# Causal attention products, a first phase without GpSimd and an early gate row in a hybrid decoder layer

## The chip, the cores and the metric

The kernel runs on one core of a Trainium2 chip. A core has five engines with a queue of instructions each: TensorE (PE, with PEld for its weight loads), VectorE (DVE), ScalarE (ACT), GpSimd (POOL) and SyncE (SP), which issues most transfers. Operands of the engines lie in SBUF; products are added up in PSUM. The metric is the device time of one execution in microseconds, the median of three runs; less is better.

## The reference

One decoder layer, 512 tokens by 1024 columns, float32:

```python
mod = silu(c) @ w_ada + b_ada
shift, scale, gate = split(mod, 3)
h = rmsnorm(x, g_pre) * (1 + scale) + shift
rq, rk, rv, rg, nq, nkv, ngl, ng = split(h @ w_in)
ret = groupnorm(retention(rotary(rq), rotary(rk), rv)) * silu(rg)     # 8 heads of 64
o_cmp = softmax(q @ kc.T, cmp_end <= tq) @ vc      # 31 compressed blocks
o_slc = softmax(q @ ks.T, tok <= tq) @ vs          # selected blocks
o_win = softmax(q @ kw.T, tq - 512 < kp <= tq) @ vw
att = (g0 * o_cmp + g1 * o_slc + g2 * o_win) * silu(ng)               # 8 heads of 64, 2 key groups
x + gate * rmsnorm(concat(ret, att) @ w_out, g_post)
```

With 512 tokens there are 8 blocks to select from and 16 may be taken, so the selected branch sees every key up to the query, as the window branch does.

## The kernel before

Every float32 operand of a large product is split into a high part `h` and a low remainder `l` that TensorE takes at full rate, and a product is three matrix multiplications: high by high, low by high, high by low. ScalarE makes the high part (a copy), VectorE or GpSimd the low one (a subtraction). So `wh_rg` and `wl_rg` are the halves of the weight `rg`, and `hh` and `hl` those of the transposed `h`.

The program is emitted by a list scheduler (`Plan`). The work stands in threads (`th_...`), each with a rank; of all that can go on, the one that can start first is emitted next. Ranks, prices and some choices of engine come from a table `T`. A step that names two engines goes to the one that the plan believes to be free sooner. Each engine then executes its own instructions in the order in which they were emitted and waits at semaphores where data or buffers are not ready. Every operation goes out through one helper, so nearly all rows name line 163 before the change and 174 after; the names of the tiles tell them apart.

The stages:

- First phase, to about 71 us. `th_ada(k)` sums column tile k of `w_ada` times silu(c) (`cs`) over eight row blocks (into `adac`, products on VectorE), transposes the sum on TensorE (`tp`), reduces it to two numbers a partition (`ab`, scale and shift); `th_prep(k)` transposes x and makes `hh` and `hl`; `th_nq_h` and `th_nq_l` multiply with the query weights (`nq`) and the weights of the compressed keys and values (`cc`). The low halves come from either GpSimd or VectorE, most from GpSimd, as do the last two steps of `ab`.
- Projections `rk`, `rv`, `rq` and `kv`, beside the two layers of compression (`w` tiles). Weights come in pieces of 256 KB through four raw buffers `wr`.
- Retention, beside the next projections.
- Attention. `th_unit(h, t)` takes query tile t of head h: scores `s` of both branches (keys `kT_h`, `kT_l`, queries `qs`; one more product with `idb` adds the causal mask `maskb`), the negated maximum `mx` on VectorE, the exponential `p` with its sum `den` on ScalarE, the division on GpSimd (`turn`), transposes on TensorE, and the split into the high and low tiles `pt..h`, `pt..l`. `th_pv(h)` multiplies these with the values `vst`, in halves of 256 queries, and with 32-row pieces of the compressed branch (`pcTh`, `pcTl`, made by `th_c`). The projections `rg` and `ng`, and later the output projection, fill TensorE between.
- The gate row. `th_gate` loads 16 pieces of `w_ada` (256 KB each) during attention into `misc`, multiplies and adds them into `gr` (GpSimd 13 times, VectorE otherwise); at the end one product with `ones` adds up the partitions.
- Output projection (`wo`, halves of `mr` for retention and `mn` for attention), root mean square, and the last additions, four query tiles one after the other.

Of the kernel before, what the change touches and what calls it, by code (L numbers as in the profile page):

```python
# [34 lines left out]
SEQ, D = 512, 1024  # L35
# [15 lines left out]
T = {'lat': 0.2, 'alt': 0.4, 'w': 1, 'post': 50, 'q': -1.8, 'var': 1.7, 'c': 1.6, 'cm': 2, 'pv': 4.5, 'gate': 300, 'kv0': 590.0, 'kv1': 105.89999999999999, 'rg': 108.5, 'ng': 601.4, 'stage': 3, 'cmp': 21, 'qs': 29.0, 'y': -0.8, 'n': -700, 'silu': 300, 'rows': 499, 'pm': 0.125, 'rgtag': 0, 'tags': 0, 'pact': 0.95, 'pv_': 1, 'pg': 1.0, 'trig': 15.0, 'ord': 0, 'att': 104.2, 'w1': 2, 'abe': 'g', 'wpre': 4, 'npj': (4, 0), 'x3': 0, 'sq3': 0, 'ada': ((0, 4, 5, 6, 7, 8), (0, 4, 6, 8), (0, 4, 8), (0, 4, 8)), 'sin': 40, 'al': 1.7, 'ld': 1, 'ad': -0.5, 'pr': 2.6, 'nh': 5.0, 'nl': 4, 'te': 'g', 'se': ('v', 'g'), 'a0': 2, 'raw': 0.12, 'half': 1, 'wg': 3}  # L51
# [6 lines left out]
class Plan:  # L58
    """A list scheduler for the order in which instructions are emitted.

    Work comes as threads: generators that yield what they need next. An engine's name (or several, to have the
    sooner one picked): the code up to the next yield emits for that engine. (get, resource, n): n free places.
    An event: that it has been set. Of all threads the one that can go on first does, the lower rank on a tie.
    """
# [3 lines left out]
    def __init__(self):  # L68
        self.cost, self.free, self.res, self.live, self.act_set = {}, {}, {}, [], None
        self.now, self.todo = 0.0, []  # L70

# [10 lines left out]
    def spawn(self, rank, gen):  # L82
        self.todo.append(("spawn", rank, gen))

# [64 lines left out]
class Engine:  # L149
    """An engine's instructions, with an estimate of what each costs for the plan."""  # L150
# [4 lines left out]
    def __getattr__(self, op):  # L155
        f = getattr(self.eng, op)

        def run(*a, **k):
            ins = [z.tensor.name for z in (*a[1:], *k.values()) if isinstance(z, bass.AP)]
            wait = T["raw"] if self.name != "pe" and self.out in ins else 0.0  # L160
            self.out = a[0].tensor.name
            self.plan.cost[self.name] = self.plan.cost.get(self.name, 0.0) + self.price(op, a, k) + wait
            return f(*a, **k)  # L163
# [6 lines left out]

def price_pe(op, a, k):
    if op == "transpose":
        return 128 * (2 if a[1].dtype == F32 else 1) / 2400
    n = size(a[2])
    if a[2].dtype == F32:
# [11 lines left out]
def price_v(op, a, k):  # L187
    n = size(a[1] if op == "tensor_reduce" else a[0])
    if op == "scalar_tensor_tensor":
        return 0.13 + n * 0.00104  # L190
    if op == "tensor_scalar" and a[1].tensor.name.split("_")[0] not in ("acc", "s", "tp", "pv"):
# [16 lines left out]
class Queue:  # L208
    """A DMA queue; plan.arrival is when the last transfer is done."""
# [13 lines left out]
def layer(ctx: ExitStack, tc: tile.TileContext, x, c, positions, w_ada, b_ada, g_pre, g_post,  # L223
# [51 lines left out]
    # ---------------------------------------------------------------- weights: float32 as hi + lo, in the order of use  # L275
# [28 lines left out]
    for k in range(KT):  # L304
        for nm, c0, n in (("nq", C_NQ, 512), ("cc", C_KV, 256)):
# [6 lines left out]
             (4, 6, 7, 8, 9, 10, 11, 12, 16, 17, 18, 19, 20, 21, 22, 23))[T["w1"]]  # L312
    for s_, (nm, u) in enumerate(MAIN):
# [13 lines left out]
    # ---------------------------------------------------------------- constants  # L327
# [5 lines left out]
    maskb, cmb, cm01 = ct("maskb", [128, 128], BF16), ct("cmb", [128, NT, 2, 32], BF16), ct("cm01", [128, 32])  # L333
# [5 lines left out]
    rs, rr = ct("rs", [128, NT, 8]), ct("rr", [40, SEQ], F32R)  # L339
    gr, sel = ct("gr", [128, D]), ct("sel", [128, 2])  # L340
# [7 lines left out]
    # =============================================================== adaLN, h, first projections  # L348
# [42 lines left out]
    for i in range(W_PRE):  # L391
# [22 lines left out]
    asel(cm01, [[-16, 32]], ALU.is_ge, 0.0, -31, 1)  # L414
    G.memset(sel, 1.0 / 64)
# [3 lines left out]
    # =============================================================== the work, as threads  # L419
    # The plan sets the order in which they are emitted.  # L420
# [9 lines left out]
    st = {}                                                    # tiles that threads share  # L430
# [1354 lines left out]
```

## Time and profile before

| | |
|---|---|
| runs, us | 394.85, 395.58, 395.92 (median 395.58) |
| span of the profiled execution, us | 392.6 |
| TensorE busy, us (share) | 369.7 (94%) |
| VectorE busy, us (share) | 290.4 (74%) |
| ScalarE busy, us (share) | 224.4 (57%) |
| GpSimd busy, us (share) | 198.8 (51%) |
| moved by DMA | 44.82 MB |

The profile shows one execution; its span, from the first to the last instruction, is 2.98 us less than the median of the runs, which holds what lies around it too. TensorE's records overlap, since its products are pipelined: how long a product occupies the engine is read from the start of one to the start of the next, not from the record's length. The chain of work that ended last is 77% TensorE.

### The profile page before, as it was taken

The numbers are of one execution on the slowest core, as the hardware profiler recorded it, in microseconds if no ns is written. First come the engines' busy times: TensorE is split into PE (matmuls) and PEld (weight loads), VectorE is DVE, ScalarE is ACT, GpSimd is POOL, SyncE is SP. The second block draws the span as 40 slices with busy tenths as digits, with TensorE's granted clock in tenths as the row PEclk, the third lists the DMA queues.
The fourth block names the chain that finished last, engine by engine and source line by source line (L and its number), as shares of the span: only waits on it lengthen the run. The fifth ranks groups of instructions, "written<-read, shape, count | busy, mean of one in ns | idle before, by whom it ended". The sixth has DMA issues, their size and how long they took to land.

```text
span 392.6 us, 7123 instructions
## 1 busy us (share of the span) xinstructions
PE 369.7 (94%) x2356; PEld 317.8 (81%) x2356; DVE 290.4 (74%) x643; ACT 224.4 (57%) x537; POOL 198.8 (51%) x332
## 2 busy tenths in 40 slices
PE   4879888999999999999999999999999999999993
PEld 1657666889999999999998888878888788777882
DVE  1598996799978756688978795488978876496532
ACT  5344545698555434367826583776786776583120
POOL 6565463214425317578735578888774443123200
PEclk9678998999999999999999999999999999999998
DMA  7999824433553454312112135423200000138341
GB/s 273 310 268 278 232 67 115 135 88 109 155 139 99 120 166 114 108 27 56 28 55 55 53 109 143 153 83 109 80 28 1 27 3 28 54 111 248 130 155 53
DMA packets 47084, 44.82 MB, mean 114 GB/s; under 512 B 5508, under 2 KB 39368, under 8 KB 47048
## 3 DMA queue, kind: packets, MB, share of 16 engines
q1 hardware_dynamic: 46984, 44.35, 38.6%
q8 instruction: 19, 0.31, 0.3%
q14 instruction: 17, 0.14, 0.1%
q10 hardware_dynamic: 64, 0.02, 0.0%
HBM read 42.26 MB, written 2.10 MB: 113 GB/s over the span
## 4 chain that ended last, share of the span: by engine, by line
PE 77%; DVE 12%; DMA 3%; ACT 3%; issue 2%; SPq 1%; POOL 1%; DVEq 0%; POOLq 0%; ACTq 0%
PE acc L163 28%; PE s L163 22%; PE tp L163 15%; PE pv L163 12%; DVE adac L163 5%; DMA xb<-in_x_dram 2%; SPq L219 1%; DMA wr_cc<-in_w_in_dram 1%; DVE fl L163 1%; DMA inv<-in_c_inv_dram 1%; ACT fl L163 1%; DVE tr L163 1%; DVE ks L163 0%; DVE wl_w L163 0%; DVE ab L163 0%
## 5 line engine op out<-in xcount | busy, mean ns | idle before, releaser
L163 POOL TENSOR_SCALAR p<-p,den 128x128 f32<-128x128 f32 (+3 forms) x64 | 36.7, 588 | 24.2 <-DVE den L163 11.7
L163 ACT ACTIVATE p<-s,mx 128x384 f32<-128x384 f32 (+3 forms) x64 | 33.7, 536 | 2.2 <-DVE mx L163 2.1
L163 DVE TENSOR_REDUCE mx<-s 128x1 f32<-128x384 f32 (+3 forms) x48 | 27.7, 593 | 3.5 <-PE s L163 3.3
L163 PE MATMUL tp<-idf,p 128*128 128x128 f32 x160 | 26.5, 276 | 0.1
L163 PE MATMUL s<-kT_h,qs 128*128 128x256 f32 (+2 forms) x64 | 25.4, 397 | 0.0
L163 DVE SCALAR_TENSOR_TENSOR adac<-ada,cs,adac 128x256 f32<-128x256 f32 x44 | 24.6, 625 | 0.0
L163 PEld LDWEIGHTS tp<-idf,p 128*128 128x128 f32 x160 | 18.4, 141 | 3.2 <-POOL p L163 0.5
L163 PE MATMUL s<-kT_l,qs 128*128 128x256 f32 (+2 forms) x64 | 20.6, 322 | 0.0
L163 PE MATMUL acc<-wh_kv,hh 128*128 128x280 f32 (+1 forms) x64 | 18.8, 294 | 0.0
L163 PE MATMUL acc<-wl_kv,hh 128*128 128x280 f32 (+1 forms) x64 | 18.3, 286 | 0.0
L163 PE MATMUL acc<-wh_kv,hl 128*128 128x280 f32 (+1 forms) x64 | 18.3, 286 | 0.0
L163 POOL TENSOR_TENSOR gr<-gr,misc 128x512 f32<-128x512 f32 x13 | 17.7, 1358 | 1.1
L163 PEld LDWEIGHTS <-idb 128*128 128x128 bf16 x84 | 8.4, 102 | 10.4 <-issue 8.4
L163 ACT ACTIVATE hh<-tp,ab 128x512 fp32r<-128x512 f32 (+1 forms) x10 | 6.8, 692 | 17.4 <-POOL ab L163 13.3
L163 POOL TENSOR_SCALAR rqd<-rq,dec 128x128 f32<-128x128 f32 x30 | 12.3, 423 | 5.2 <-PE tp L163 4.5
L163 PE MATMUL s<-maskb,idb 128*128 128x128 bf16 x64 | 14.7, 230 | 0.0
L163 DVE TENSOR_TENSOR spl<-s,sph 128x384 fp32r<-128x384 f32 (+1 forms) x24 | 13.7, 595 | 1.3 <-ACT sph L163 1.2
L163 PE MATMUL acc<-hh,wh_ng 128*128 128x512 f32 x32 | 14.6, 455 | 0.0
L163 PE MATMUL acc<-hh,wh_rg 128*128 128x512 f32 x32 | 13.6, 425 | 0.0
L163 ACT ACTIVATION_READ_ACCUMULATOR p<-s,mx 128x1 f32 x64 | 13.4, 209 | 0.0
L163 ACT CAST pt10h<-tp 128x384 fp32r<-128x384 f32 (+1 forms) x16 | 8.6, 536 | 8.4 <-PE tp L163 8.4
L163 PEld LDWEIGHTS s<-kT_h,qs 128*128 128x128 f32 x64 | 12.5, 195 | 1.0 <-ACT p L163 0.2
(463 smaller groups left out, 1468.2 us busy)
## 6 DMA issues: line engine op xcount, KB each, us to landing
ada<-in_w_ada_dram SPq DMA_DIRECT2D x8, 512.0 KB, 5.0
misc<-in_w_ada_dram SPq DMA_DIRECT2D x16, 256.0 KB, 2.8
wor<-in_w_out_dram SPq DMA_DIRECT2D x16, 256.0 KB, 2.7
ada<-in_w_ada_dram SPq DMA_DIRECT2D x12, 256.0 KB, 5.5
wr_nq<-in_w_in_dram SPq DMA_DIRECT2D x8, 256.0 KB, 4.4
wr_rk<-in_w_in_dram SPq DMA_DIRECT2D x8, 256.0 KB, 3.1
wr_w<-in_cmp_w_k_dram SPq DMA_DIRECT2D x8, 256.0 KB, 2.7
wr_rv<-in_w_in_dram SPq DMA_DIRECT2D x8, 256.0 KB, 2.8
```

What stands on the lines that cost most here:

```text
L163: return f(*a, **k)
L219: self.eng.dma_start(dst, src)
```

## The change

- **Table and plan.** About a dozen numbers of `T` are new, among them ranks that move whole stages; the plan now also counts the time in which a VectorE operation and a GpSimd operation exclude each other (`take_port`).
- **First phase.** The low halves of `nq` and `cc`, the halves `hl` and the end of `ab` are fixed on VectorE. For k of 3 and up one of the eight products goes to TensorE, and the sum is taken over the partitions by a product with `ones` in place of transposes and a reduction.
- **Gate row.** Its 16 loads stand in the stream of weights now, behind pieces of `rk` to `rq`, in the `wr` buffers (`ga`). `th_ga` adds them up, 13 pairs and a product on GpSimd and two operations on VectorE. Eight products with one column of `ones` then give the gate as 8 columns, to which `b_ada` and `g_post` are applied; `th_grow` makes the row again from 8 scaled identities and two products. Four loads of rows are gone, two small ones are added at the start.
- **Scores.** The mask is no product any more. One VectorE operation reads scores and mask, writes their negated sum to `p` and its minimum to `mx`; the exponential then reads `p`. For t of 0 and 1 both branches share two products.
- **Numerators.** All queries of a head in one bank, key tile k only for the queries that see it (512, 384, 256, 256 columns), one branch after the other; the compressed branch is one product with zero-padded values `vz`, from four transposes a query tile.
- **Late weights.** The low halves of `rg`, `ng` and `wo` prefer GpSimd.

The diff, cut:

```diff
+    def take_port(self, name, c):
+        t = max(self.free.get(name, 0.0), self.now) + self.cost.get(name, 0.0)
+        wait = max([e - t for s, e in self.port["g" if name == "v" else "v"] if s <= t < e] + [0.0])
+        self.port[name] = self.port[name][1:] + [(t + wait, t + wait + c)]
+        return wait
...
+            if 4 * s_ + kk in GA_AT:
+                j = len(GA)
+                GA[j] = w_add(f"ga{j}", (1, 512), [(wa[:, j % 8, None, 2 * D + j // 8 * 512:2 * D + j // 8 * 512 + 512], 512)])
...
-        e = yield "g", "v"
-        sub(e, hl[k], h32, hh[k])
+        yield "v"
+        sub("v", hl[k], h32, hh[k])
...
-            e = yield T["se"] if i > T["wg"] else "g"
+            e = yield "v" if i < 2 * KT else T["se"] if i < WC["rg", 0, 0] else T["sl"]
             sub(e, t_[1], w_raw[i], t_[0])
...
-            e = yield "v", "g"
+            e = yield T["so"]
             sub(e, lo, wor[i], hi)
...
     def th_c(t):
+        yield e_gfree
...
-        for g in range(2):
-            tr(p_[:, tsl(g)], gr[:, t * 256 + g * 128:t * 256 + (g + 1) * 128], idf)
+        for m in range(4):
+            tr(p_[:, tsl(m)], cd[:, 2 * m:2 * m + 2].rearrange("p h c n -> p (h c n)"), idf)
...
-            mm(s_[:, n - 128:n], idb, maskb, False, True)
...
+        def lower(b, s_):
+            V.tensor_tensor_reduce(p_[b], s_, maskd[0][:, SEQ - n:], -1.0, 3e38, ALU.add, ALU.min, mx[:, b:b + 1])
+        def numer(b):
+            z = p_[b]
+            exp_(z, z, bias=mx[:, b:b + 1], scale=-1.0, accum_out=den[:, b:b + 1])
...
+            mm(s_, q, kT_h[:, g, :, 0:n], True, False)
+            mm(s_, q, st["kT_l"][:, g, :, 0:n], False, True)
...
-                for k in range(2 + 2 * z):
-                    for p in range(2):
-                        mm(o[:, sl], vst[:, k, b, g, :], PH[z][b][p][:, k, :], b == 0 and k == 0 and p == 0, False)
-                if b:
-                    r0 = (h % 4) * 32
-                    for p in range(2):
-                        mm(o[:, sl], vcst[r0:r0 + 32, g, :], pcT[g][p][r0:r0 + 32, sl], False, p == 1)
+        mm(o, vz[0][:, 2 * (h % 2) + g], pcT[0][:, h // 2], True, False)
+            for k in range(NT):
+                q0 = min(128 * k, 256)
+                for p in range(2):
+                    mm(o[:, q0:], vst[:, k, b, g, :], PH[b][p][:, 384 * k + q0:384 * k + SEQ], False, b + p == 2 and k == NT - 1)
...
+    def th_ga(i, w):
+        f, j = divmod(i, KT)
+        sl, ga = slice(f * 512, (f + 1) * 512), w_raw[w][:, 0]
+        if j == 0:
+            {"g": G, "v": V}[e].tensor_scalar(gr[:, sl], ga, cs[:, 0:1], 1.0, ALU.mult, ALU.mult)
+        elif e == "g":
+            G.tensor_scalar(ga, ga, cs[:, j:j + 1], 1.0, ALU.mult, ALU.mult)
+            G.tensor_tensor(gr[:, sl], gr[:, sl], ga, ALU.add)
+        else:
+            V.scalar_tensor_tensor(gr[:, sl], ga, cs[:, j:j + 1], gr[:, sl], ALU.mult, ALU.add)
...
+        for k in range(KT):
+            mm(b[:, k:k + 1], gr[:, k * 128:(k + 1) * 128], ones[:, 0:1], True, True)
```

VectorE in the first phase, column k = 6, before: the reduction of the column before it, then the six products into the two halves of the sum, and the addition of the halves. The low halves `hl` and `wl_cc` of the same time are in GpSimd's queue.

```order
L163 TENSOR_REDUCE ab_598<-tp_577 128x2
L163 SCALAR_TENSOR_TENSOR adac0_588<-ada6_475,cs_107,adac0_588 128x256
L163 SCALAR_TENSOR_TENSOR adac1_589<-ada6_475,cs_107,adac1_589 128x256
L163 SCALAR_TENSOR_TENSOR adac0_588<-ada6_475,cs_107,adac0_588 128x256
L163 SCALAR_TENSOR_TENSOR adac1_589<-ada6_475,cs_107,adac1_589 128x256
L163 SCALAR_TENSOR_TENSOR adac0_588<-ada6_475,cs_107,adac0_588 128x256
L163 SCALAR_TENSOR_TENSOR adac1_589<-ada6_475,cs_107,adac1_589 128x256
L163 COPY pT_106<-tp_624 128x32
L163 TENSOR_TENSOR adac0_588<-adac0_588,adac1_589 128x256
```

VectorE at the same column after the change, with both steps of `ab` ahead of it.

```order
L174 TENSOR_TENSOR ab_589<-tp_560,smT_171 128x2
L174 TENSOR_SCALAR ab_589<-ab_589,smT_171 128x1
L174 SCALAR_TENSOR_TENSOR adac0_577<-ada6_463,cs_106,adac0_577 128x256
L174 SCALAR_TENSOR_TENSOR adac1_578<-ada6_463,cs_106,adac1_578 128x256
L174 SCALAR_TENSOR_TENSOR adac0_577<-ada6_463,cs_106,adac0_577 128x256
L174 SCALAR_TENSOR_TENSOR adac1_578<-ada6_463,cs_106,adac1_578 128x256
L174 SCALAR_TENSOR_TENSOR adac0_577<-ada6_463,cs_106,adac0_577 128x256
L174 TENSOR_TENSOR wl_nq5_583<-wr_nq5_497,wh_nq5_582 128x512
L174 COPY pT_105<-tp_605 128x32
L174 TENSOR_TENSOR hl5_88<-h32_599,hh5_80 128x512
L174 TENSOR_TENSOR wl_cc5_624<-wr_cc5_525,wh_cc5_623 128x256
L174 TENSOR_TENSOR adac0_577<-adac0_577,adac1_578 128x256
```

The reduction and one product are gone, and three low halves have moved in between the products and the last addition.

TensorE in attention, before: the end of one head's numerators (`pt01`, the low and high tile of a branch), the compressed pieces, transposes of `p`, and four scores with their masks.

```order
L163 MATMUL pv<-pcTh_3039,vcst 128x256
L163 MATMUL pv<-pcTl_3040,vcst 128x256
L163 MATMUL tp<-idf,p 128x128 x2
L163 MATMUL s<-kT_h,qs_852 128x384
L163 MATMUL s<-kT_l,qs_852 128x384
L163 LDWEIGHTS idb
L163 MATMUL s<-maskb,idb 128x128
L163 MATMUL s<-kT_h,qs_852 128x512
L163 MATMUL s<-kT_l,qs_852 128x512
L163 LDWEIGHTS idb
L163 MATMUL s<-maskb,idb 128x128
```

TensorE at a like place after the change: one head's first branch as a whole, transposes, and the scores of t = 3 and of a unit whose branches share their products.

```order
L174 MATMUL pv<-pcT,ph 128x512
L174 MATMUL pv<-ph,vst 128x512 x2
L174 MATMUL pv<-ph,vst 128x384 x2
L174 MATMUL pv<-ph,vst 128x256 x4
L174 MATMUL tp<-idf,p 128x128 x5
L174 MATMUL s<-kT_h,qs_848 128x512
L174 MATMUL s<-kT_l,qs_848 128x512
L174 MATMUL s<-kT_h,qs_848 128x256
L174 MATMUL s<-kT_l,qs_848 128x256
```

The masks and their weight loads are gone, the compressed pieces are one product at the head's start, and a branch's numerators stand together. After the last head's second branch 15 products of the output projection on retention's halves follow, and then the first on attention's (`mnh`).

GpSimd beside the projection `rk`, before: rotated keys (`rk`), blocks for the compression (`flr`) and one low half of `rv`.

```order
L163 TENSOR_TENSOR rk<-rra,rrb 128x256 x2
L163 TENSOR_TENSOR flr<-fl_0_811,flr 128x8x64
L163 TENSOR_TENSOR rk<-rra,rrb 128x256 x4
L163 TENSOR_TENSOR wl_rv_1341<-wr_rv_1255,wh_rv_1340 128x512
L163 TENSOR_TENSOR rk<-rra,rrb 128x256 x2
```

GpSimd at the same place after the change, with pairs that scale a piece of the gate's weights (`wr_ga`) and add it to `gr`.

```order
L174 TENSOR_TENSOR rk<-rra,rrb 128x256 x2
L174 TENSOR_SCALAR wr_ga_1176<-wr_ga_1176,cs 128x512
L174 TENSOR_TENSOR gr<-gr,wr_ga_1176 128x512
L174 TENSOR_TENSOR rk<-rra,rrb 128x256
L174 TENSOR_SCALAR wr_ga_1232<-wr_ga_1232,cs 128x512
L174 TENSOR_TENSOR gr<-gr,wr_ga_1232 128x512
L174 TENSOR_TENSOR rk<-rra,rrb 128x256
L174 TENSOR_SCALAR wr_ga_1282<-wr_ga_1282,cs 128x512
L174 TENSOR_TENSOR gr<-gr,wr_ga_1282 128x512
L174 TENSOR_TENSOR rk<-rra,rrb 128x256
```

A pair of the gate's sum now stands before nearly every rotated tile.

## Rows read from the trace of the kernel before

**Rows 1.** The page's first part: busy time, share of the span and instructions of each engine.

```profile
PE 369.7 (94%) x2356; PEld 317.8 (81%) x2356; DVE 290.4 (74%) x643; ACT 224.4 (57%) x537; POOL 198.8 (51%) x332
```

**Rows 2.** Busy time by stretch: the stretch and its length, then busy time (and instructions) of PE, PEld, DVE, ACT and POOL, PE's granted clock as a share of full speed, the DMA engines' busy share, and GB/s.

```profile
0.00:71.00 71.00, 56.03 (x231) 41.05 (x232) 51.22 (x104) 34.59 (x73) 38.79 (x68) 0.88 0.77 220
71.00:110.00 39.00, 37.13 (x313) 36.12 (x312) 37.17 (x73) 28.65 (x56) 14.06 (x14) 1.00 0.42 117
110.00:140.00 30.00, 30.00 (x254) 29.50 (x253) 23.76 (x54) 16.30 (x34) 10.45 (x12) 1.00 0.41 117
...
215.00:300.00 85.00, 84.94 (x531) 69.02 (x530) 65.61 (x162) 59.91 (x174) 64.00 (x92) 1.00 0.28 88
300.00:345.00 45.00, 45.00 (x285) 36.92 (x284) 30.90 (x76) 30.00 (x83) 14.35 (x22) 1.00 0.09 30
```

**Rows 3.** Timeline of PE in the first phase: start, length, engine, operation, tiles, shape; in brackets the idle time before it and what ended it.

```profile
60.57 0.41 PE L163 MATMUL tp<-idf,adac 128*128 128x128 f32 x2 [2.25 <-DVE adac L163]
...
71.16 0.28 PE L163 MATMUL acc<-wh_rk,hh 128*128 128x256 f32 x1
```

**Rows 4.** Timeline of POOL in the first phase, with the same columns.

```profile
39.97 1.28 POOL L163 TENSOR_TENSOR hl<-h,hh 128x512 fp32r<-128x512 f32 x1 [0.44 <-ACT h L163]
...
62.27 0.26 POOL L163 TENSOR_SCALAR ab<-ab,smT 128x1 f32<-128x1 f32 x1
```

**Rows 5.** Timeline of DVE in the first phase, with the same columns.

```profile
17.38 0.16 DVE L163 TENSOR_TENSOR ab<-tp,smT 128x2 f32<-128x2 f32 x1 [3.42 <-PE tp L163]
...
17.71 0.61 DVE L163 TENSOR_SCALAR adac<-ada,cs 128x256 f32<-128x256 f32 x2
...
36.75 0.42 DVE L163 TENSOR_REDUCE ab<-tp 128x2 f32<-128x256 f32 x1 [0.80 <-PE tp L163]
...
40.06 1.47 DVE L163 TENSOR_TENSOR adac<-adac,adac 128x256 f32<-128x256 f32 x1
...
42.07 0.68 DVE L163 TENSOR_TENSOR wl_nq<-wr_nq,wh_nq 128x512 fp32r<-128x512 f32 x1
42.67 0.41 DVE L163 TENSOR_REDUCE ab<-tp 128x2 f32<-128x256 f32 x1
43.01 1.26 DVE L163 SCALAR_TENSOR_TENSOR adac<-ada,cs,adac 128x256 f32<-128x256 f32 x3
...
62.64 0.42 DVE L163 TENSOR_TENSOR wl_cc<-wr_cc,wh_cc 128x256 fp32r<-128x256 f32 x1
62.97 0.33 DVE L163 SCALAR_TENSOR_TENSOR tr<-kf,tr 128x168 f32<-128x168 f32 x1
```

**Rows 6.** Timeline of PE in attention, from 240.65 to 249.43 us, with the same columns.

```profile
240.65 0.39 PE L163 MATMUL acc<-hl,wh_rg 128*128 128x512 f32 x1
240.88 0.39 PE L163 MATMUL acc<-hh,wh_rg 128*128 128x512 f32 x1
...
246.67 0.28 PE L163 MATMUL pv<-pt01h,vst 128*128 128x256 f32 x1
246.79 0.28 PE L163 MATMUL pv<-pt01l,vst 128*128 128x256 f32 x1
247.00 0.38 PE L163 MATMUL pv<-pcTh,vcst 32*128 32x256 f32 x1
247.22 0.27 PE L163 MATMUL pv<-pcTl,vcst 32*128 32x256 f32 x1
247.42 0.44 PE L163 MATMUL tp<-idf,p 128*128 128x128 f32 x2
247.62 0.42 PE L163 MATMUL s<-kT_h,qs 128*128 128x384 f32 x1
247.87 0.33 PE L163 MATMUL s<-kT_l,qs 128*128 128x384 f32 x1
248.05 0.23 PE L163 MATMUL s<-maskb,idb 128*128 128x128 bf16 x1
248.09 0.48 PE L163 MATMUL s<-kT_h,qs 128*128 128x512 f32 x1
...
248.68 0.36 PE L163 MATMUL s<-kT_h,qs 128*128 128x256 f32 x1
...
249.43 0.39 PE L163 MATMUL tp<-idf,p 128*128 128x128 f32 x2
```

**Rows 7.** Groups of instructions over the whole run: operation, tiles, shapes, count, then busy time and mean ns of one, then the idle time before them and what ended it. The first is DVE's maxima, then low halves on DVE, then ACT's read of its accumulator.

```profile
L163 DVE TENSOR_REDUCE mx<-s 128x1 f32<-128x384 f32 (+3 forms) x48 | 27.7, 593 | 3.5 <-PE s L163 3.3
...
L163 DVE TENSOR_TENSOR wo<-wor,wo 128x512 fp32r<-128x512 f32 x13 | 10.2, 790 | 3.9 <-ACT wo L163 3.8
...
L163 DVE TENSOR_TENSOR wl_ng<-wr_ng,wh_ng 128x512 fp32r<-128x512 f32 x8 | 7.2, 895 | 4.2 <-ACT wh_ng L163 4.2
...
L163 DVE TENSOR_TENSOR pt10l<-tp,pt10h 128x512 fp32r<-128x512 f32 x8 | 5.5, 690 | 2.4 <-ACT pt10h L163 2.3
...
L163 ACT ACTIVATION_READ_ACCUMULATOR p<-s,mx 128x1 f32 x64 | 13.4, 209 | 0.0
```

**Rows 8.** The gate's sum on POOL, as groups with the same columns, and one low half on DVE from the timeline of that time.

```profile
L163 POOL TENSOR_TENSOR gr<-gr,misc 128x512 f32<-128x512 f32 x13 | 17.7, 1358 | 1.1
...
L163 POOL TENSOR_SCALAR misc<-misc,cs 128x512 f32<-128x512 f32 x13 | 9.5, 729 | 1.8 <-DMA misc<-in_w_ada_dram 1.8
...
239.19 1.09 DVE L163 TENSOR_TENSOR wl_ng<-wr_ng,wh_ng 128x512 fp32r<-128x512 f32 x1 [0.38 <-ACT wh_ng L163]
```

More of the change, by code (lines that the diff above doesn't have):

```diff
@@ L161, in run @@
             self.out = a[0].tensor.name
-            self.plan.cost[self.name] = self.plan.cost.get(self.name, 0.0) + self.price(op, a, k) + wait
+            c = self.price(op, a, k) + wait
+            if self.name in self.plan.port and shares_port(self.name, op, a):
+                c += self.plan.take_port(self.name, c)
+            self.plan.cost[self.name] = self.plan.cost.get(self.name, 0.0) + c
             return f(*a, **k)
@@ L381, in layer @@
     S.dma_start(small[16:32], b_ada[:, 0:2 * D].rearrange("b (k p) -> (b k) p", p=128))
+    S.dma_start(small[32:40], b_ada[:, 2 * D:].rearrange("b (k p) -> (b k) p", p=128))
+    S.dma_start(small[40:48], g_post.rearrange("b (k p) -> (b k) p", p=128))
     xa = [big("xa"), big("xb")]
@@ L482, in th_small @@
         P.set(e_sm)
+        P.set(e_cons)
     def th_pos():
@@ L711, in th_nq_l, with x2_get, x2_put @@
             P.set(e)
-    cc32 = {}
+    cc32, x2_t, x2_free, x2_at = {}, [], [0, 1, 2, 3], {}
+    def x2_get(key=None):
+        if not x2_t:
+            x2_t.append(an.tile([128, 4, SEQ], F32, name="x2", tag="x2"))
+        x2_at[key] = x2_free.pop(0)
+        return x2_t[0][:, x2_at[key]]
+    def x2_put(key):
+        x2_free.append(x2_at.pop(key))
+        P.put("x2")
     def th_fin(i):
@@ L1321, in th_c @@
             yield z
-        if not pcT:
+        if t == 0:
             yield get("x2", 4)
-            pcT.extend([an.tile([128, SEQ], F32R, name=f"pcT{p}{g}", tag="x2", bufs=4) for p in "hl"] for g in range(2))
+            pcT.append(an.tile([128, 4, SEQ], F32R, name="pcT", tag="x2"))
+            P.set(e_px)
+        yield e_px
+        yield e_at
+        yield get("cd")
+        cd = st["misc"][:, len(cds) % 2].rearrange("p (h c n) -> p h c n", h=8, c=2)
+        cds.append(cd)
+        e = yield "g", "v"
+        {"g": G, "v": V}[e].tensor_tensor(cd, bc(p3, [32, 8], [0, 2], [1, 32]), bc(den, [1, 8], [0, 2], [0, 32]), ALU.mult)
         yield get("tp")
@@ L1368, in th_at @@
         P.set(e_rr)
+        yield e_vc
+        yield "g"
+        vz.append(ph[:, :, 1280:1408])
+        G.memset(vz[0].bitcast(F32), 0.0)
+        for r in range(2):
+            G.tensor_copy(vz[0][64 * r:64 * r + 64, 2 * r:2 * r + 2], vcst[64 * r:64 * r + 64].bitcast(F32))
+        P.set(e_vz)
     def th_unit(h, t):
-        g, n, nn, z = h // 4, 128 * (t + 1), max(128 * (t + 1), 256), t // 2
-        for i in range(max(t, 1) + 1):
+        g, n = h // 4, 128 * (t + 1)
+        for i in range(t + 1):
             yield e_k[i]
```

261 lines of the change are left out of this document (131 added, 130 removed).

## Prediction

> **What bounds the kernel now.** I read the page's shares first, then the stretches, then single timelines. TensorE is busy for 94% of the span [rows 1], and the windows show where the rest is: it works 56.03 of the first 71.00 us, 37.13 of the 39.00 up to 110, and all the time after that [rows 2]. So two things can shorten the run: fewer TensorE passes after 110 us, or an earlier end of the first phase. In the first phase the work goes round a loop: VectorE sums column k of the modulation, TensorE transposes the sum and waits for it (2.25 us before 60.57 [rows 3]), VectorE reduces it, GpSimd finishes `ab`, ScalarE makes `hh`, and TensorE multiplies. The last `ab` is done at 62.27 + 0.26 = 62.53 [rows 4], and the first product of the next projection starts at 71.16, 8.6 us later [rows 3].
>
> VectorE is slowed there by GpSimd. Alone, a product of the sum takes 1.26 / 3 = 0.42 us [rows 5]. The final addition, two tiles of SBUF, began at 40.06 and took 1.47 us, while GpSimd's `hl` ran from 39.97 to 41.25 [rows 4, 5]: the addition did its own work after GpSimd had ended. The Trainium skill ("SBUF — State Buffer", section "SBUF: two separate sides") states that VectorE with two SBUF inputs and GpSimd exclude each other for a whole instruction over a shared pair of ports. By that rule, and by this row, taking GpSimd out of the first phase is right, and giving it more to do later is not free.
>
> **First phase: -6.3 us.** After the sum at 17.38 VectorE would do, without GpSimd beside it: 37 products of 0.42 = 15.5; 14 low halves of 512 columns (`wl_nq`, `hl`) at 42.67 - 42.07 = 0.60, 8.5; 15 short operations (final additions, `wl_cc`, two reductions) at about 0.36 (62.97 - 62.64 = 0.33 and 0.42), 5.4; 8 pairs that finish `ab` at 17.71 - 17.38 = 0.33, 2.6; and some 13 pieces of angle work of 0.33 to 0.42, about 4.8 [rows 5]. That is 36.8, so the last `ab` falls at 54.2 if VectorE never waits. It will wait for TensorE as it does now (up to 0.80 us a column [rows 5]): 7 times 0.6 gives 58.4. With the old lag of 8.6 the projection starts between 62.8 and 67.0. I take the middle, 64.9, against 71.16: -6.3. Bounds: -2, if TensorE or the loads, which keep the DMA engines 0.77 busy over these 71 us [rows 2], set the pace; -9, if nothing waits. The other edits here (one of eight products on TensorE for k of 3 and up, sums by a product with ones) lie inside these counts. Two more small loads on ScalarE's queue at the start (`b_ada`, `g_post` as columns) and the four row loads that go at the end cost and give nothing: what needs them is far behind them.
>
> **TensorE passes in attention: -14.8 us.** From start to start a 512-column product takes 0.23 us, a 256-column one 0.12, and a 384-column one 0.18 [rows 6].
> - Scores. For t of 2 and 3, a branch with its mask takes 248.68 - 248.09 = 0.59 where two plain products need 0.46, so 32 branches save 0.12 each = 3.8. A unit of t = 0 or 1 takes 249.43 - 248.68 = 0.75 [rows 6] and becomes two products of 256 (0.24) or of 512 (0.46): 8 x (0.51 + 0.29) = 6.4. The first product behind transposes is longer than the next by 0.25 - 0.18 = 0.07 [rows 6], and I take back 16 such, 1.2. Together -9.0.
> - Numerators. 24 products of 256 a head, 2.88, and two pairs of 32-row ones, each 247.42 - 246.79 less the ordinary 0.12, so 0.51 [rows 6]: 3.91 a head. After: 4 x 0.232 + 4 x 0.18 + 8 x 0.12 + 0.232 = 2.84. Eight heads: -8.5.
> - Added: 8 transposes of the compressed branch at 0.10 to 0.11 (247.42 to 247.62 for two [rows 6]), +0.9; 8 one-column sums of the gate in float32, which I take as two passes of a transpose's length each, +1.8.
>
> The bounds are -11 (only what the masks and the 32-row products cost comes back) and -16.5 (no switch between shapes costs anything, the gate's sums go at half that).
>
> That saving counts only if TensorE is truly full. The records show starts 0.23 apart without a break, and no wait noted beside them [rows 6]. The Trainium skill ("Perfetto Trace Analysis", section "Identifying the Most-Contended Engine") holds that busy time of matrix products is a poor measure of that and that the busy share of weight loads is the better one. That share is 81% here [rows 1], which by this rule would leave room on TensorE, and part of a saving would turn to idle time; that is the third rival below.
>
> **VectorE in attention: hidden.** The numerators' exponentials on ScalarE are as many as before, reading SBUF where they read PSUM. VectorE, between 215 and 345 us, is busy 65.61 + 30.90 = 96.5 of 130 [rows 2]. The maxima leave (27.7), `wl_ng` leaves (7.2), and about ten more low halves of 0.79 (7.9) [rows 7]: 53.7 stay. The new step writes, from PSUM and a mask in SBUF, a whole row to SBUF, and then its minimum. No row shows it. The nearest is the low half of a transposed tile, 0.69 for 512 columns [rows 7], about 0.49 over the four widths; an accumulator's read is 0.21 on ScalarE [rows 7]. I take 0.70, 64 times = 45. From below: 0.49, no read. VectorE then has 99 of the 113 to 115 us that TensorE needs. It sets the pace from (114 - 53.7) / 64 = 0.94 us a step.
>
> **Middle, 71 to 140 us: +3.** Thirteen pairs on GpSimd (0.73 + 1.36 = 2.1 each [rows 8]) come here, 27 us beside its 14.06 + 10.45 [rows 2], and VectorE has 37.17 of 39.00 us up to 110 filled [rows 2]. What one meeting costs: `wl_ng` took 1.09 at 239.19 beside this same work [rows 8], 0.4 over its 0.69; the addition above lost 1.05. Some 15 of the 26 operations fall before 110; at 0.3 each that is 4.5, less 1.8 idle, about 3. Bounds 0 (they fall into gaps) and +8 (26 x 0.4 less the idle). The 16 loads move no byte that was not moved before; DMA is at 0.42 there [rows 2] and the weights behind them wait four slots for GpSimd, which is the same price. The compressed branch now waits for the gate's sum, since both use `gr`; the sum ends with this stage and the branch begins after it, so I price the wait at nothing, and a late sum is part of rival 2.
>
> **End of attention: +2.5.** The last head's second branch now stands right behind its own transposes: a copy and a subtraction of about 0.69 each [rows 7] lie open, 1.4. Behind it 15 products (3.5 us) cover the join, gating and splitting, some seven steps of 0.69 = 4.8: 1.3 open. The bounds are 0 and +6, the latter with the last `wo` halves on GpSimd at about 1.36 each [rows 8] on the path.
>
> **Sum.** 392.6 - 6.3 - 14.8 + 3.0 + 2.5 = 377.0 for the span. The median of the runs is 2.98 over the profiled span, and I keep that: 380.0 us.
>
> **Rivals.**
> 1. *Nothing new is late.* Middle and end cost nothing: 380.0 - 5.5 = 374.5, and down to 370 with the better bounds. For it: GpSimd has idle time in the middle; against: VectorE hardly has any.
> 2. *GpSimd is late where the work went.* Middle +8 and end +6, by the exclusion seen in rows 4 and 5: 374.5 + 14 = 388.5. For it: the two work side by side in every stage after 71 us now; against: at 239.19 the price was 0.4, not 1.
> 3. *TensorE was not full.* Its saving becomes waiting for scores, numerators and transposes; only the first phase remains: 392.6 - 6.3 + 3.0 = 389.3. Against: rows 6.
> 4. *The first phase gains nothing,* as loads or TensorE pace it: 380.0 + 6.3 = 386.3.
> 5. *Slower: the new VectorE step sets the pace of attention.* At x us a step attention lasts 53.7 + 64x. The 15.6 us that the forecast gains are gone when it lasts 114 + 15.6 = 129.6, at x = 1.19; at 1.25 the time is 395.6 + 4.1 = 399.7. For it: the operation is in no row, it writes a full row and a minimum; against: it would have to take 2.4 times the 0.49 of the nearest row.
>
> **How the numbers follow.** Forecast 0.43, rival 1 0.22, rival 2 0.17, rival 3 0.05, rival 4 0.05, rival 5 0.06, and 0.02 for a sum that ends within 0.3% of before, which is about what a measurement of this kernel can tell from no change. Faster: 0.92. The range runs from 370.5 (rival 1 with nearly all good bounds) to 390.0: it leaves out rival 5, no change, the upper half of rival 3, about 0.07 of rival 2 and 0.02 of rival 1.
>
> **What would show it.** First phase: the 71.16 start at 63 to 67, no addition of VectorE over 0.5 us there. Attention: no `maskb` product, a t = 0 or 1 unit of two products 0.12 or 0.23 apart, TensorE without idle time; the new step at 0.5 to 0.8 us. Middle: VectorE operations stretched beside `gr`, and TensorE idle for some 3 us more than now. End: gaps of 1 to 2 us before the last numerators and before the first `mnh` product. I am wrong if TensorE shows idle time spread through attention with VectorE or GpSimd named before it, or if the first projection still starts near 71.

## The result and the profile after

| | before | after |
|---|---|---|
| median, us | 395.51 (4 runs) | 399.6 (4 runs, 398.69 to 401.24) |
| span of the profiled execution, us | 392.6 | 396.9 |
| first product of the projection `rk`, us | 71.16 | 63.63 |
| last product of the output projection starts, us | 386.16 | 390.28 |

The change makes the kernel slower: the ratio of the times is 1.0128, 95% interval 1.0084 to 1.0172. The forecast was 380.0 with a range of 370.5 to 390.0. The median stands 2.7 us over the span, much as before.

The same stretches as in [rows 2], now of the changed kernel (busy time of PE, PEld, DVE, ACT, POOL; granted clock; DMA share; GB/s):

```profile
0.00:71.00 71.00, 60.67 (x324) 48.42 (x324) 53.67 (x139) 41.96 (x86) 13.29 (x41) 0.98 0.82 237
71.00:110.00 39.00, 33.38 (x272) 32.30 (x271) 34.34 (x54) 23.43 (x47) 28.37 (x27) 0.96 0.46 138
110.00:140.00 30.00, 29.01 (x238) 27.97 (x237) 24.54 (x47) 11.88 (x26) 22.67 (x23) 1.00 0.54 162
...
215.00:300.00 85.00, 79.99 (x432) 66.11 (x432) 53.38 (x174) 57.96 (x150) 58.37 (x89) 0.98 0.14 41
300.00:345.00 45.00, 40.24 (x215) 32.77 (x214) 33.55 (x114) 41.17 (x105) 28.87 (x37) 0.96 0.16 54
```

TensorE, which had next to no idle time between 110 and 345 us, now stands still in every stage. VectorE, the rival's suspect for attention, is less busy between 215 and 300 us than before (53.38 for 65.61).

The first phase, on VectorE at a later column (timeline: start, length): five products take 2.06 us, 0.41 each, and the last addition 0.42, where [rows 5] had 1.47.

```profile
44.14 2.06 DVE L174 SCALAR_TENSOR_TENSOR adac<-ada,cs,adac 128x256 f32<-128x256 f32 x5
46.12 0.69 DVE L174 TENSOR_TENSOR wl_nq<-wr_nq,wh_nq 128x512 fp32r<-128x512 f32 x1
...
47.75 0.42 DVE L174 TENSOR_TENSOR adac<-adac,adac 128x256 f32<-128x256 f32 x1
```

The new step of VectorE, as groups by width (busy time, mean ns): 0.284 to 0.688 us, and 0.082 for its minimum. The groups of the narrowest and the widest stand here; together the 64 steps of all four widths are 35.3 us.

```profile
L174 DVE CUSTOM_DVE_ANT_0 p<-s,misc 128x512 f32<-128x512 f32 x16 | 10.9, 688 | 2.0 <-PE s L174 1.7 <-PE tp L174 0.2
...
L174 DVE DVE_READ_ACCUMULATOR2_ANT mx<- 128x1 f32 x64 | 5.3, 82 | 0.0
L174 DVE CUSTOM_DVE_ANT_0 p<-s,misc 128x128 f32<-128x128 f32 x16 | 4.2, 284 | 1.6 <-PE tp L174 1.1 <-POOL misc L174 0.2
```

What the work itself costs on TensorE, worked out from both traces as the time from each product's start to the next, summed by kind, in us:

| kind | before | after | difference | forecast |
|---|---|---|---|---|
| scores | 28.74 | 22.76 | -6.0 | -9.0 |
| numerators and compressed pieces | 32.86 | 24.30 | -8.6 | -8.5 |
| transposes of the compressed branch | 1.11 | 1.91 | +0.8 | +0.9 |
| gate | 0.92 | 3.02 | +2.1 | +1.8 |

So the first phase gives 7.5 us and these products 11.6. The last product would start at 386.2 - 19.1 = 367.1; it starts at 390.3. Some 23 us are lost elsewhere. TensorE's waits of over 0.15 us between the first product of `rk` and that last one add up to 1.9 us before and to 19.5 after; most of the rest is the half clock that follows three of them (last section). I found three places. The first is the stream of weights. The waits of SyncE's queue between 60 and 160 us (total, times, longest) begin with the sum of the gate on GpSimd, which has to read a raw buffer before the next load may use it:

```profile
SPq L245 <- POOL gr L174: 28.6, 13, 3.1
SPq L245 <- DMA wr_ga<-in_w_ada_dram: 10.1, 9, 2.1
SPq L245 <- DVE wl_w L174: 8.7, 6, 3.4
```

In the kernel before that queue waited 9.8 us for GpSimd in the same stretch (4.4, 3.9 and 1.5 us, by tile). In the same stage TensorE waits 3.03 us for `ks`, which stands on VectorE behind a low half and an addition that are each stretched (1.24 and 1.19 us; 0.69 and 0.68 where the sum is left out, below) while GpSimd adds and rotates:

```profile
93.80 1.24 DVE L174 TENSOR_TENSOR wl_rv<-wr_rv,wh_rv 128x512 fp32r<-128x512 f32 x1
...
94.96 1.19 DVE L174 TENSOR_TENSOR x<-x,pT 128x496 f32<-128x496 f32 x1
...
97.36 0.66 PE L174 MATMUL tp<-idf,rk 128*128 128x128 f32 x2 [3.03 <-DVE ks L174]
```

The second is at 228 us, the third between 321 and 337 us. First the timeline of the second, of POOL, ACT and PE:

```profile
229.73 1.26 POOL L174 CAST ph<-misc 8x512 fp32r<-8x512 f32 x2
231.03 0.63 ACT L174 ACTIVATE misc<-rq 128x512 f32<-128x512 f32 x1 [4.92 <-POOL ph L174]
...
231.71 1.05 PE L174 MATMUL tp<-sel,misc 128*128 128x2 f32 x8 [3.49 <-ACT misc L174]
```

`th_at` stages the row selector in piece 2 of `misc` (before: piece 3, which now holds the mask). `th_var` writes its squares for the last pair of heads into that same piece 2, so ScalarE has to wait until GpSimd has set up the mask, the selector and two clearings and has copied the selector out. Nothing in the computation asks for that wait. Then the third, ACT, POOL and PE:

```profile
331.51 1.28 ACT L174 ACT_TABLE_LOAD   x1
331.57 1.27 POOL L174 TENSOR_TENSOR wo<-wor,wo 128x512 fp32r<-128x512 f32 x1 [0.39 <-ACT wo L174]
...
332.80 0.63 ACT L174 ACTIVATE ng<-ng 128x512 f32<-128x512 f32 x1
332.82 1.86 POOL L174 TENSOR_SCALAR p<-p,den 128x512 f32<-128x512 f32 x2
333.34 0.46 ACT L174 CAST ph<-tp 128x384 fp32r<-128x384 f32 x1
...
334.82 0.63 PE L174 MATMUL tp<-idf,p 128*128 128x128 f32 x4 [2.46 <-POOL p L174]
...
336.55 1.28 ACT L174 ACT_TABLE_LOAD   x1
```

The last product of the projection `ng` starts at 316.7 us now and at 339.0 before, so its silu falls between the exponentials. Between 300 and 345 us ScalarE changes its tables (its functions' tables are loaded anew, `ACT_TABLE_LOAD`) at 321.58, 324.90, 331.51 and 336.55 us; in the kernel before it did so once, at 342.11. The profile names GpSimd's division as the last thing waited for; the copy `ph`, which frees the bank for the transposes, ends only 1 us earlier, and stands behind a table load. Which one is to blame is an experiment's question.

### The profile page after: what moved, and what is told of

It reads as the page before. It is cut to its first block, busy times and chain, and to the rows that moved or that the text cites. A ratio compares the mean times of both kernels' runs of the same rounds, so it can differ in the third digit from the quotient of the medians.

```text
span 396.9 us, 6892 instructions
## 1 busy us (share of the span) xinstructions
PE 360.6 (91%) x2226; PEld 312.3 (79%) x2226; DVE 283.0 (71%) x702; ACT 233.7 (59%) x535; POOL 209.6 (53%) x330
## 5 line engine op out<-in xcount | busy, mean ns | idle before, releaser
L174 DVE TENSOR_TENSOR ph<-tp,ph 128x384 fp32r<-128x384 f32 (+2 forms) x64 | 30.2, 488 | 14.0 <-ACT ph L174 13.8
L174 ACT ACTIVATE p<-p,mx 128x128 f32<-128x128 f32 (+3 forms) x64 | 35.7, 562 | 0.0
L174 ACT CAST ph<-tp 128x384 fp32r<-128x384 f32 (+2 forms) x64 | 26.1, 425 | 15.8 <-PE tp L174 15.3
L174 DVE CUSTOM_DVE_ANT_0 p<-s,misc 128x128 f32<-128x128 f32 (+3 forms) x64 | 29.7, 485 | 5.1 <-PE tp L174 2.5
L174 PE MATMUL pv<-ph,vst 128*128 128x256 f32 (+2 forms) x128 | 24.1, 329 | 0.9 <-ACT ph L174 0.7
L174 PEld LDWEIGHTS pv<-ph,vst 128*128 128x128 f32 x128 | 21.0, 189 | 3.3 <-ACT ph L174 0.9
L174 POOL TENSOR_TENSOR wo<-wor,wo 128x512 fp32r<-128x512 f32 x14 | 18.3, 1307 | 7.3 <-ACT wo L174 5.9
L174 POOL TENSOR_TENSOR gr<-gr,wr_ga 128x512 f32<-128x512 f32 x13 | 19.7, 1512 | 1.1
L174 PE MATMUL s<-kT_h,qs 128*128 128x512 f32 (+2 forms) x48 | 19.9, 416 | 0.1
L174 POOL TENSOR_SCALAR wr_ga<-wr_ga,cs 128x512 f32<-128x512 f32 x13 | 10.9, 839 | 16.1 <-DMA wr_ga<-in_w_ada_dram 12.9
L174 PE MATMUL s<-kT_l,qs 128*128 128x512 f32 (+2 forms) x48 | 17.6, 369 | 0.0
L174 ACT ACT_TABLE_LOAD x10 | 12.8, 1283 | 6.6 <-DVE gr L174 3.7
L174 DVE SCALAR_TENSOR_TENSOR adac<-ada,cs,adac 128x256 f32<-128x256 f32 x39 | 16.1, 479 | 0.0
```

## The experiments

Theory: the gain is lost in three separate waits, and each costs a stretch at half clock too. Rivals: the new order of the stages is the loss, and a removed wait comes back at the next place; or GpSimd itself, by its time and by what VectorE yields to it. "In its own order" means that the changed kernel's sequence of the plan's choices is replayed, so that every engine has its instructions in the same order and only the edit differs. Medians stand beside the changed kernel's 399.6 and about 395.4 for the kernel before. The 399.6 comes from four runs between 398.69 and 401.24 us, so a difference to it is sure to about 1 us.

In a held order TensorE has the same 2226 products in the same sequence, so the traces tell where time comes back: how much earlier than in the changed kernel one and the same product starts, in us, named by its start there. (In the two runs with the silu moved, the order of some forty products between the last two columns differs; the products named are the same.)

| run | 63.63 (first of `rk`) | 140.96 | 227.83 (before the wait for `misc`) | 239.05 | 316.74 (last of `ng`) | 390.28 (last) |
|---|---|---|---|---|---|---|
| staging | 0.45 | 1.99 | 1.86 | 7.18 | 7.21 | 6.08 |
| without the gate's sum | -0.25 | 7.32 | 7.38 | 6.34 | 6.37 | 5.85 |
| GpSimd's work without the buffers | -0.23 | 5.45 | 5.54 | 4.40 | 4.43 | 4.45 |
| staging and the gate's sum on VectorE | 0.57 | 5.82 | 5.92 | 11.24 | 11.25 | 11.28 |
| the silu behind | 0.59 | 0.44 | 0.47 | 0.47 | 0.43 | 5.87 |
| all three, held | -0.23 | 5.37 | 5.42 | 10.74 | 10.71 | 16.11 |

Each row is one profiled execution. The staging run gained 1.5 us up to 140.96, where nothing had been edited, so a step of that size is scatter. In the second and third row about 1 us is lost again between 227.83 and 239.05: the wait for `misc` is as long as in the changed kernel (3.5 us), but the granted clock is lower (0.96 for 0.98 between 215 and 300 us).

**Staging.**

```diff
-        sT = st["misc"][0:8, 2].rearrange("p (m q) -> p m q", m=4)
+        sT = st["misc"][0:8, 0].rearrange("p (m q) -> p m q", m=4)
```

> The changed kernel in its own order, but the small table for the row selector is staged in a piece of misc that ScalarE doesn't write next (piece 0 for piece 2). Theory (the changed kernel's gain is eaten by several waits on GpSimd, and each long one costs TensorE's clock too): TensorE's 3.5 us wait near 228 us goes, and with it the stretch at half clock behind it; 4 to 5 us less than the changed kernel, about 395. Rival (the new order of the stages itself is the loss, and a removed wait comes back at the next place): under 1 us less, 398.5 to 400.

Measured 392.82 us, 6.8 less; ratio to before 0.996 (0.9927 to 0.9992). TensorE's granted clock between 215 and 260 us is 1.00 again and its busy time 43.51 of 45 (41.51 after). The wait and its stretch at half clock go, as the theory said, though the gain is more than its 4 to 5 us. In place, from 227.83 to 239.05, it is 5.3 us (7.18 - 1.86; 5.3 in the two other runs with this edit), which is the wait of 3.49 and some 1.7 of half clock; in this trace 1.9 more came before the place of the edit and 1.1 is lost again behind 316.74 (granted clock 0.92 for 0.96 between 300 and 345 us). So one tile's place was worth more than the whole measured loss of 4.1.

```profile
215.00:260.00 45.00, 43.51 (x238) 35.75 (x237) 25.55 (x79) 30.97 (x72) 34.17 (x54) 1.00 0.16 47
```

**Without the gate's sum.**

```diff
-        if j == 0:
+        if j:
+            pass
+        elif j == 0:
             {"g": G, "v": V}[e].tensor_scalar(gr[:, sl], ga, cs[:, 0:1], 1.0, ALU.mult, ALU.mult)
```

> The changed kernel in its own order, its 16 gate loads kept, but 14 of the 16 pieces aren't multiplied and added (so the gate isn't the reference's); their raw buffers come free as soon as they have landed. Theory: the gate's sum on GpSimd holds the raw buffers and the weights behind them come late; without it TensorE's waits between 90 and 140 us go, 5 to 7 us less than the changed kernel, 392 to 395. Rival (the loads themselves, or the order, make the weights late): 0 to 1.5 us less.

Measured 393.57 us, 6.0 less, as the theory had it. The 16 loads are still in this run, and TensorE is busy for 37.03 us from 71 to 110 and for all of the 30.00 up to 140, as in the kernel before (37.13 and 30.00), so the loads as such cost nothing that shows. Of its waits there one is left, 1.9 us for `ks`.

**Late low halves on VectorE.**

```diff
             e = yield T["se"] if i < WC["rg", 0, 0] else T["sl"]
+            e = "v" if i >= WC["rg", 0, 0] else e
...
             e = yield T["so"]
+            e = "v"
```

> The changed kernel in its own order, with the low halves of rg, ng and wo on VectorE at the same places. Theory: GpSimd's divisions no longer stand behind low halves of 1.3 us; TensorE's waits for p between 318 and 336 us (4 us, and half clock behind the last) go, 4 to 6 us less than the changed kernel, 394 to 396. Rival (VectorE is full with its new step, or the waits are ScalarE's): no gain, or up to 3 us more, 399 to 403.

Measured 398.99 us, no gain that shows. TensorE waits at the same places for as long; only the name beside the waits has changed, from `p` on GpSimd (first line, the changed kernel between 300 and 345 us) to `ph` and `den` on VectorE (second line, this run up to 360 us), all behind ScalarE. The theory of GpSimd's divisions falls.

```profile
PE tp L174 <- POOL p L174: 3.9, 3, 2.5
```

```profile
PE tp L234 <- DVE ph L234: 3.8, 4, 2.4
```

**The first phase alone,** in the kernel before.

```diff
-T = {..., 'abe': 'g', ..., 'npj': (4, 0), ...}
+T = {..., 'abe': 'v', ..., 'npj': (4, 0, 0, 1, 1, 1, 1, 1), ...}
...
-        e = yield "g", "v"
-        sub(e, hl[k], h32, hh[k])
+        yield "v"
+        sub("v", hl[k], h32, hh[k])
...
-            e = yield T["se"] if i > T["wg"] else "g"
+            e = yield "v" if i < 16 else T["se"]
```

> The kernel before with the first phase of the changed one alone (low halves and ab on VectorE, one of eight products on TensorE from k = 3). Theory: the 7.5 us that the changed kernel has won at the start of the projection rk are kept to the end, since what loses them is elsewhere; 387.5 to 389. Rival (the lead is lost to loads and to the order of the projections whatever comes later): 393 to 396.

Measured 387.5 us, 0.9808 of before (0.9758 to 0.9858). What the first phase wins is kept to the end: in its profiled run, the slowest of the four, `rk` starts 4.9 us earlier than before (66.22) and the last product 4.9 us earlier too (381.28).

**The silu of `ng` behind the last exponential,** planned anew; the order is the changed kernel's up to the place where that silu stood.

```diff
-    e_s, e_exp, e_att = evs(2, 16), Ev(32), evs(8)
+    e_s, e_exp, e_att = evs(2, 16), Ev(64), evs(8)
```

> The changed kernel, but the silu of ng waits for all 64 exponentials of attention and not for the first 32, so that ScalarE's tables change once there and not four times. Theory: between 318 and 337 us ScalarE is the late one (four table loads of 1.28 us, and the copies of the transposed tiles stand behind them); three loads go and TensorE's waits there with them: 3 to 5 us less than the changed kernel, 394.5 to 396.5. Rival (GpSimd's divisions or VectorE are as late, or the silu is then late at the end): within 1 us of the changed kernel, 398.5 to 400.5.

Measured 393.17 us, 6.4 less. One table load is left there, at 340.87 us, and TensorE is busy for 44.09 of the 45 us up to 345 (40.24 after), at full clock:

```profile
300.00:345.00 45.00, 44.09 (x245) 36.19 (x244) 36.77 (x119) 39.62 (x107) 31.97 (x41) 1.00 0.16 54
```

The low halves stayed on GpSimd here. So the late one was ScalarE, and the profile's "GpSimd `p`" was only the last of several that were late together. In place, behind 316.74, the gain is 5.4 us. The plan also ordered some forty of TensorE's products there anew, and no run parts that from the table loads.

**Staging and the gate's sum on VectorE,** in its own order.

```diff
         e = yield "g", "v"
+        e = "v"
         if j == 0:
```

> The changed kernel in its own order with the other staging piece, and with the gate's sum on VectorE at the same places (one operation a piece and not two on GpSimd). Theory (two separate losses): the gains add up less what 13 operations of some 0.66 us cost a VectorE that is 88% busy between 71 and 110 us: 6.8 and 3 to 6 less than the changed kernel, 387 to 390. Rival (both losses eat the same slack further on): 391.5 to 393.

Measured 387.42 us, 12.2 less, and 5.4 beyond the staging alone, where leaving the sum out gave 6.0. In place it is 5.3 up to 140.96 and 5.3 at the wait for `misc`: two separate losses.

**All three, planned anew.** The edits are those of the two kernels above, the sum's engine fixed in the `yield`.

> The changed kernel with all three: other staging piece, gate's sum on VectorE, silu of ng behind the last exponential, in an order that the plan makes anew. Theory: the three losses are separate, 399.6 - 6.8 - 5 - 4, so 384 (381 to 387), and below the first phase alone (387.5). Rival (the plan's new order loses elsewhere what is mended here): 387 to 392.

Measured 401.99 us. Neither theory nor rival allowed for that. With one engine's choice fixed the plan orders everything after it differently; in the trace TensorE waits for `wl_rq` (2.9 us, 0.5 in the changed kernel), for `gat` (2.8, where it did not), for `p` (5.8, then 3.9) and, in spite of the other staging piece, for `misc` (2.6, then 3.5).

**All three, in a held order** (the replayed order of the kernel with the silu behind).

> The three mended in a held order: the order of the run with the silu behind all exponentials, with the other staging piece and the gate's sum on VectorE at the same places, nothing planned anew. Theory (three separate losses of 6.8, 5.4 and 6.4 us, and the 402 of the freshly planned one was its order): 399.6 - 18.6 = 381 (379 to 383). Rival (what is mended last comes back at the next place): 385 to 388.

Measured 382.59 us, 0.9682 of before (0.9649 to 0.9716): 17.0 of the 18.6 us are there together; in place they are 5.6, 5.3 and 5.4. Against the kernel planned anew it is 19.4 us less with the same edits, and that difference is order alone.

**The ranks of the kernel before,** with the staging and the silu mended, planned anew. Six of the ten ranks stand here; the edits for the staging and the silu are those above.

```diff
-T = {..., 'var': 4.47, 'c': -6.65, ..., 'pv': 6.2, ..., 'kv0': 105.7, 'kv1': 566.4, 'rg': 122.1, ...}
+T = {..., 'var': 1.7, 'c': 1.6, ..., 'pv': 4.5, ..., 'kv0': 590.0, 'kv1': 105.89999999999999, 'rg': 108.5, ...}
```

> The changed kernel with the other staging piece and the silu behind the last exponential, its gate's sum on GpSimd as it was, and with the ranks of the kernel before (var, c, pv, kv0, kv1, rg, cmp, n, att, sin). Theory (the waits named, not the new ranks, are the loss): 399.6 - 6.8 - 4, so 387 to 391. Rival (the new ranks are themselves a loss): 380 to 386.

Measured 392.4 us, over both ranges. The old ranks bring no gain here: by the sum of the two mends the new ones should stand at 386 to 387 (399.6 - 6.8 - 6.4), which was not run. But this order was planned anew, which cost 19.4 us in the run with all three, so whether the new ranks are a part of the loss stays open.

**The low halves once more,** on VectorE, in the kernel with the three mended.

> As the kernel with the three mended in a held order, and the low halves of rg, ng and wo on VectorE at the same places. Theory (with ScalarE's table loads gone, GpSimd's divisions behind low halves of 1.3 us are the next late ones): 2 to 4 us less than that kernel, 377 to 379. Rival (VectorE's own queue is as late): within 1 us of it, 380 to 382.

Measured 382.55 us: nothing. Which engine takes the late low halves matters neither before nor after the mend.

**GpSimd's work without the buffers,** in its own order.

```diff
         e = yield "g", "v"
+        ga = bc(ones, [0, 4], [1, 128]) if e == "g" and j else ga
...
-            G.tensor_scalar(ga, ga, cs[:, j:j + 1], 1.0, ALU.mult, ALU.mult)
+            G.tensor_scalar(gr[:, sl], ga, cs[:, j:j + 1], 1.0, ALU.mult, ALU.mult)
```

> The changed kernel in its own order; GpSimd does the same 13 pairs of operations, of the same size, but on constants and not on the loaded pieces (so the gate isn't the reference's): the raw buffers come free when they have landed, and GpSimd waits for no load, while its time and what VectorE has to give way to stay. Theory A (raw buffers held for GpSimd make the weights late): 4 to 6 us less than the changed kernel, 393.5 to 395.5, as without the sum. Theory B (GpSimd's time, and VectorE waiting beside it, is the price): 0 to 2 us less, 397.5 to 399.6.

Measured 394.13 us, 5.5 of the 6.0 us that leaving the sum out gave. GpSimd is busier than in the changed kernel (31.36 and 25.08 us for 28.37 and 22.67), and TensorE has most of the time back (35.88 and 30.00 for 33.38 and 29.01; 37.03 and 30.00 without the sum):

```profile
71.00:110.00 39.00, 35.88 (x304) 34.92 (x303) 36.58 (x61) 26.54 (x52) 31.36 (x29) 1.00 0.49 151
110.00:140.00 30.00, 30.00 (x254) 29.53 (x253) 27.54 (x52) 13.16 (x28) 25.08 (x24) 1.00 0.61 177
```

SyncE's queue has no wait for GpSimd among its longest any more:

```profile
SPq L305 <- DVE wl_w L234: 18.2, 11, 3.4
SPq L305 <- DMA wr_ga<-in_w_ada_dram: 16.8, 10, 2.8
```

The price was the raw buffers that waited for GpSimd and GpSimd that waited for loads (this run takes both away), and much less its work and what VectorE yields to it: VectorE still gives way here (0.90, 1.20 and 1.04 us for a low half, the addition and a low half before `ks`; 0.69, 0.68 and 0.69 without the sum). For that the medians leave some 0.6 us and the two traces 1.9 up to 140.96, which is near the scatter. TensorE's wait for `ks` is in every run with the sum left out, on constants or on VectorE (1.9 to 2.6 us, 3.03 in the changed kernel), so the order makes it, and GpSimd only makes it longer. The rule of the Trainium skill ("SBUF — State Buffer", section "SBUF: two separate sides") holds where the first phase shows it (an addition of 1.47 us beside GpSimd, 0.42 without), but its price in the middle is small.

## Why the prediction was wrong

- **First phase, -6.3: right.** It is -7.5 (71.16 to 63.63; 64.9 was forecast), and 387.5 us for it alone. VectorE's operations have the lengths that the sum used, and the last `ab` is done at 56.28 us, between the 54.2 and the 58.4 of the prediction; the lag behind it is 7.4 us and not 8.6.
- **TensorE's passes, -14.8: mis-sized in one term.** Numerators, transposes and gate are within 0.3 us as differences (the numerators take 1.6 us more than the sum had, on both sides). The scores give 6.0 and not 9.0. By the plain lengths of [rows 6] (0.12, 0.18 and 0.23 a product) the 48 pairs would take some 18.7 us, and they take 22.76. I took the longer first product back for 16 pairs; 18 stand behind transposes or the products with `sel` and cost 1.6 us, so that part of the sum was right. In the lines below it is 0.26 us to the next start behind the transposes at 334.82, and 0.18 where the product before is a numerator of retention. The other 2.5 us had no term: 0.9 are two pairs at 317.7 us beside the waits there, 0.9 six products at half clock, 0.4 one product behind the gate row's. Most of that belongs to the waits below.

```profile
222.01 0.35 PE L174 MATMUL s<-kT_h,qs 128*128 128x384 f32 x1
222.19 0.34 PE L174 MATMUL s<-kT_l,qs 128*128 128x384 f32 x1
...
335.20 0.42 PE L174 MATMUL s<-kT_h,qs 128*128 128x384 f32 x1
335.46 0.34 PE L174 MATMUL s<-kT_l,qs 128*128 128x384 f32 x1
```

- **VectorE in attention: right that it is hidden.** The new step takes 35.3 us in all; 45 was taken. Rival 5, the only slower one, was the wrong reason for the right sign: 0.55 us a step, not 1.19. (The time of rival 3, 389.3, lacks the 2.98 between span and median that the forecast has; with it the rival is at 392.3, outside the range.)
- **Middle, +3: too small, by the wrong mechanism.** It is about 6. The prediction priced what VectorE yields to GpSimd, and called the four buffers "the same price". The buffers and the loads were most of it (5.5 of 6.0).
- **The step that failed: what was not in the sum.** Two waits had no term, the one for `misc` and those behind ScalarE's table loads, worth 6.8 and 6.4 us by the medians, 5.3 and 5.4 in place, half clock included. The prediction looked at VectorE's busy time in attention, found its 99 of 113 to 115 us enough, and passed ScalarE with the sentence that its exponentials are as many as before. They are, but a silu had come between them, which the order of ScalarE would have told; and a staging tile had come to lie where another thread writes, which the line of `th_at` and that of `th_var` tell when read side by side. The prediction's own sign of being wrong came, idle time in attention with GpSimd named before it (3.9 us), though the one named wasn't the late one.
- **End, +2.5: about right.** The last branch waits 0.68 us for the copy and 0.23 for the subtraction, and 0.70 for `o32n` behind it, 1.6 in all:

```profile
354.16 0.49 PE L174 MATMUL pv<-ph,vst 128*128 128x512 f32 x1 [0.68 <-ACT ph L174]
354.89 1.34 PE L174 MATMUL pv<-ph,vst 128*128 128x512 f32 x7 [0.23 <-DVE ph L174]
...
357.63 0.72 PE L174 MATMUL pv<-wo,mrh 128*128 128x512 f32 x2 [0.70 <-DVE o32n L174]
```

With the three mended the kernel takes 382.59 us, 2.6 over the forecast, and that it comes so near is partly luck: the first phase gave 1.2 us more, TensorE's passes 3.2 less, and what is still lost, 7.1 us at the last product (374.18 for 367.1), stands where 5.5 was priced for the middle and the end. Of the 23.2 us lost, the three mends give back 16.1 in the trace. Of the 7.1 left, 6.2 are waits of TensorE (8.1 us in the mended kernel, 1.9 before): 2.6 for `ks`, 1.7 at the last branch, the others under 1 us each, in retention and in attention. They were not tried one by one.

## What to carry to other kernels

Where one engine is full, a change that frees it is worth what it saves less the waits that it uncovers, and these aren't found in the busy shares of the others: read the new order of each engine for what has come between (a table change, a load behind a slow reader of a shared buffer), and every tile that has moved for who else writes there. A wait of 3.5 us on TensorE was worth 5.3 here, with the half clock behind it. And where a planner makes the order, test an edit in a held order first, since the plan's answer to a small edit can be larger than the edit.

## What the runs showed of the hardware that was not expected

After each of three long waits TensorE was granted half its clock, for some 3 us. The windows around them show it (granted clock third from the end): 0.50 behind the wait at 94 us, 0.66 and then 0.91 over four microseconds each behind the one at 228, and 0.61 behind that at 332.

```profile
98.00:100.00 2.00, 2.00 (x12) 2.00 (x11) 1.59 (x3) 1.72 (x4) 1.92 (x3) 0.50 0.13 43
228.00:232.00 4.00, 0.51 (x4) 0.29 (x3) 0.70 (x4) 0.97 (x2) 2.87 (x6) 1.00 0.21 61
232.00:236.00 4.00, 4.00 (x18) 3.46 (x19) 2.37 (x9) 3.13 (x13) 2.29 (x2) 0.66 0.24 69
236.00:240.00 4.00, 4.00 (x17) 2.91 (x16) 1.51 (x6) 1.81 (x5) 0.00 (x0) 0.91 0.00 0
332.00:336.00 4.00, 1.51 (x8) 1.28 (x9) 2.23 (x7) 3.99 (x9) 3.76 (x4) 0.96 0.21 71
336.00:340.00 4.00, 4.00 (x16) 3.26 (x15) 2.76 (x11) 3.72 (x10) 1.12 (x2) 0.61 0.23 66
```

Four microseconds at 0.66 and four at 0.91 are 1.7 us of full speed lost, so the wait of 3.49 us at 228 comes to 5.2, and the runs where it was taken away gave back 5.3 in place. The other surprise is how cheap the new step's minimum is: 82 ns, where ScalarE's read of an accumulator took 209 [rows 7]. The Trainium skill ("ScalarE activation tables: per-element evaluation and per-set limits", section "What a function is on this engine") gives 1283 ns for a change between functions of different sets; the trace agrees, with 1.28 us a load, and three loads too many and what they held up cost 6.4 us here by the medians, 5.4 in place, the new order behind them included.
